# A two-layer hybrid decoder trunk: first stage in four blocks at once, pooling products later, transposes a tile behind, embedding weights loaded first

## The chip, the cores and the metric

The kernel runs on one core of a Trainium2 chip. The metric is device time in microseconds (us) from one launch. The engines are PE (TensorE, matmuls, with its weight loads PEld), DVE (VectorE), ACT (ScalarE), POOL (GpSimd) and SP (SyncE, which issues all DMAs). Each engine runs its own queue in order. Where an instruction waits for a semaphore, all that stands behind it in that queue waits too.

## The reference

All data are float32. The sequence has 1024 tokens of width 1024; there are two layers, one even and one odd.

```python
def reference(x, p, positions, norm_g, ple_w_gate, ple_w_proj, ...):
    h = x
    for i in range(DEPTH):                       # DEPTH = 2
        hn = rmsnorm(h, norm_g[i])
        m = even_layer(hn, ...) if i % 2 == 0 else odd_layer(hn, ...)
        h = h + m
        h = h + jax.nn.sigmoid(h @ ple_w_gate[i]) * (p[i] @ ple_w_proj[i])
    return h
```

The even layer multiplies the normalised input by one wide matrix, `ev_w_in`. The first 512 columns feed a pooling mixer: window means over 2, 4, 8 and 16 tokens minus the token, a small 64x64 product for each of four groups, a scale and a SiLU gate. The rest feeds six heads of differential attention: two softmaxes a head, subtracted with a factor lambda, with normalised and partly rotated queries and keys, an RMS norm and a gate. The odd layer has four heads of latent attention (low-rank queries and keys, `z = hn @ w_in` cut into 256 + 128 + 64 columns, normalised, multiplied up again) and four heads of a gated delta rule: a causal convolution, a triangular system of 64x64 per chunk (`solve(I + strict(kk * gamma * beta), [v*beta, k*beta*exp(gc)])`) and a recurrence over 16 chunks. After each layer comes a gated embedding, whose product `p[i] @ ple_w_proj[i]` is 1024x256 by 256x1024.

## The kernel before

The width or the tokens lie on 128 partitions, and an output tile is 128x512 (one bank of PSUM). Float32 products are made of three matmuls on a rounded high part and a low part of both operands: `mm3` (L141 to L144) issues high x high, high x low and low x high. `split` (L131 to L138) makes the parts: ACT casts the high part (L134, or L137 with a scale), DVE subtracts it (L135, or L138). `wload` (L151) loads 128x512 weight tiles through a pool of four raw buffers and splits them; the DMA is L158. `proj_T` and `proj_tok` run over the eight (or two) pieces of the contracted dimension with `mm3`, so that a 128x512 output costs 24 matmuls (6 for the embedding).

PSUM banks come from small pools by name: `acc` (2), `s` (2), `x` (2), `tr` (1) and `o` (1). A tile that asks for a bank waits until the reader of the bank's last content is done.

A scheduler sets the order in each engine's queue when the kernel is built: it follows the dependences and its own estimate of when each result is ready, and not the order of the program. Generators (`even_proj`, `even_attn`, `ple_proj` and others) issue a piece of work per step, and `step(...)` advances them in turn; this gives the scheduler the pieces to interleave.

The first stage (L354 to L376) multiplies the input by the first 512 columns of `ev_w_in`, transposed: four output blocks of 128 columns (`first`, `second`), for the first and the second half of the tokens. The first half takes each of eight pieces `k` as it arrives and does 12 matmuls with it. The second half does three blocks and then the fourth with `proj_T`, on a bank of pool `acc`. Column sums of squares (L333) give the norm of each token through `token_rstd` (L178, ones-vector matmuls L182) and `token_row` (L185, a matmul L190 and a copy L191 that spread it along a row). `pool_in` (L345) multiplies a block with that row (L347, L350) and makes the gate (tanh L351, product L352). `even_pool` (L417) makes the window sums on POOL (L421), copies on ACT (L430), corrects them on DVE (L431 to L433) and multiplies by the group matrices on PE (L437). The head projections `even_proj` (L442) follow: four steps of two token tiles, each with one bank of `acc` that ACT and DVE read (L459 to L463; L463 is the last reader).

`ple_proj` (L579) makes the embedding product: it splits the inputs `pT`, then for each of two column groups loads two weight tiles and makes 8 outputs, each copied (L127) and stored (L595). `latent` (L750) makes the latent columns of a token tile: three activations (L760 to L764), a Newton iteration, two scalings (L771), three transposes on PE (L774) and their splits. `block_solve` (L983) inverts 32x32 triangular blocks for all chunks with 62 DVE operations (L994, L996) and stores them as `xinv` (L997); `gdn_solve` (L1002) reads blocks of it back into `U` (L1010) and assembles each 64x64 and 128x128 solution with small matmuls and copies. `mla_prep` (L1127) loads latent queries and keys as `zq` (L1135, L1136) and transposes them on PE (L1144).

Of the kernel before, what the change touches and what calls it, by code (L numbers as in the profile page):

```python
# [10 lines left out]
F32 = mybir.dt.float32  # L11
# [45 lines left out]
def trunk_kernel(ctx, tc, a, out, layers=2):  # L57
# [120 lines left out]
    def token_rstd(sums):  # L178

        ps = bank("o")  # L180
        for c in range(4):
            pe.matmul(ps[:, c:c + 1], sums[:, c * P:(c + 1) * P], ones[:, 0:1], start=True, stop=True)  # L182
        return mean_rsqrt(ps[:, 0:4], 4, D, "tok")

    def token_row(dst, cols, dg):  # L185
# [3 lines left out]
        ps = bank("o")  # L189
# [132 lines left out]
    def load_x(h, k, sums):  # L322
        raw = slots[h][k]
        dma.dma_start(raw, a["xT"][k * P:(k + 1) * P, h * 512:(h + 1) * 512])
        hi, lo = xt(), xt()
        split(hi, lo, raw, ng[:, k:k + 1])
        hn[k][h] = (hi, lo)
# [7 lines left out]
    def finish_x(h, sums):  # L335
        set_rstd(0, h, token_rstd(sums))
        token_row(rrow[h], rstd[0][:, 4 * h:4 * h + 4], T("sq", 3))
# [17 lines left out]
    first, w_pool = [bank(n) for n in ("acc", "acc", "s", "s")], []  # L355
    for k in range(KC):
        load_x(0, k, sums[0])
        w_pool += wload(a["ev_w_in"], 0, 512, row=k, nk=1)
        for j in range(4):
            q = slice(j * P, j * P + P)  # L360
            mm3(first[j], w_pool[k][0][:, q], w_pool[k][1][:, q], *hn[k][0], k == 0, k == KC - 1)
    second = [bank(n) for n in ("x", "x", "tr")]
    dma.dma_start(cst[:, P:C_END], a["cst"][:, P:C_END])
    for k in range(KC):
        load_x(1, k, sums[1])
        for j in range(3):
            q = slice(j * P, j * P + P)
            mm3(second[j], w_pool[k][0][:, q], w_pool[k][1][:, q], *hn[k][1], k == 0, k == KC - 1)
        if k == 2:
            finish_x(0, sums[0])  # L370
        if k > 3:
            pool_in(first[k - 4], k - 4, 0)
# [964 lines left out]
```

## Time and profile before

| what | value |
|---|---|
| median of 3 runs | 1472.44 us (1470.59 to 1477.74) |
| profiled execution | 1472.82 us |
| its span | 1471.1 us |
| mean granted clock of PE | 0.993 |
| busy: PE, DVE, ACT, POOL | 1415.7, 977.9, 664.6, 195.9 us |
| matmuls | 7447 |

A row of a timeline has the start in us from the span's start, the busy time in us, the engine, the source line, the operation, output and inputs with their shape, and in brackets how long the engine had been idle before it and what released it. `SPq` is the issue of a DMA by SP. A row of stretches has for each engine the busy time, then the granted clock of PE as a share of full, the share of time the DMA engines were busy, and GB/s. A waits row has the total in us, how often, and the longest.

### The profile page before, as it was taken

The page shows a single profiled execution, that of the slowest core. Times are in us where ns is not written, and L with a number is a line of the kernel's source. Part 1 is how long each engine was busy: PE and PEld are TensorE (multiplying, and loading weights), DVE is VectorE, ACT ScalarE, POOL GpSimd, SP SyncE. Part 2 cuts the span into 40 slices and gives each one's busy share as a digit, 9 for nine tenths or more (in the row PEclk, how much of TensorE's full clock was granted, in tenths as well). Part 3 has the DMA queues.
Part 4 walks back from the last instruction along what each step waited for, and adds up shares of the span by engine and source line. Part 5 has one row for each costly group of instructions (what it writes and reads, how often), then busy time and mean ns, then how long its engine had stood idle before and what let it go on. Part 6 is the DMA issues. An engine that isn't in the chain of part 4 may idle for free. (4 is left out here: it accounts for less than half of the span.)

```text
span 1471.1 us, 22586 instructions
## 1 busy us (share of the span) xinstructions
PE 1415.7 (96%) x7447; PEld 1153.8 (78%) x7447; DVE 977.9 (66%) x2853; ACT 664.6 (45%) x1662; POOL 195.9 (13%) x341
## 2 busy tenths in 40 slices
PE   8999999999999999999999999999989999999998
PEld 6677888888887778887777878778768888887876
DVE  6756766666667785366676788997557887633342
ACT  6335555565656732343554543434334455722220
POOL 0321101111011000022015621210000000000021
PEclk9999999999999999999999999999999999999999
DMA  6223424232333563333424433343676634443332
GB/s 225 61 70 103 108 51 108 51 108 51 101 101 99 160 200 109 108 121 119 103 70 165 181 107 102 99 134 110 214 250 195 204 124 135 129 137 104 126 108 86
DMA packets 127605, 181.51 MB, mean 123 GB/s; under 512 B 28393, under 2 KB 55297, under 8 KB 127489
## 3 DMA queue, kind: packets, MB, share of 16 engines
q1 hardware_dynamic: 127488, 180.08, 39.7%
q8 instruction: 59, 0.97, 0.3%
q14 instruction: 58, 0.47, 0.1%
HBM read 108.20 MB, written 52.95 MB: 110 GB/s over the span
## 5 line engine op out<-in xcount | busy, mean ns | idle before, releaser
L143 PE MATMUL acc<-wl,x 128*128 128x512 f32 (+1 forms) x576 | 229.5, 399 | 3.2 <-DVE wl L135 3.2
L142 PE MATMUL acc<-wh,x 128*128 128x512 f32 (+1 forms) x576 | 231.0, 402 | 0.7 <-DVE g L463 0.6
L144 PE MATMUL acc<-wh,x 128*128 128x512 f32 (+1 forms) x576 | 228.0, 396 | 0.0
L142 PE MATMUL acc<-x,wh 128*128 128x512 f32 x504 | 202.9, 403 | 6.1 <-ACT wh L134 4.6
L144 PE MATMUL acc<-x,wl 128*128 128x512 f32 x504 | 200.2, 399 | 3.6 <-DVE wl L135 3.3
L143 PE MATMUL acc<-x,wh 128*128 128x512 f32 x504 | 199.8, 397 | 0.0
L135 DVE TENSOR_TENSOR wl<-raw,wh 128x512 fp32r<-128x512 f32 (+2 forms) x184 | 124.5, 698 | 31.8 <-ACT wh L134 30.2
L134 ACT CAST wh<-raw 128x512 fp32r<-128x512 f32 (+2 forms) x184 | 105.9, 600 | 69.4 <-PE acc L143 22.6
L143 PEld LDWEIGHTS acc<-wl,x 128*128 128x128 f32 x576 | 109.2, 190 | 26.9 <-DVE wl L135 4.2
L142 PEld LDWEIGHTS acc<-wh,x 128*128 128x128 f32 x576 | 109.2, 190 | 24.4 <-DVE g L463 1.4
L144 PEld LDWEIGHTS acc<-wh,x 128*128 128x128 f32 x576 | 109.0, 189 | 22.5
L142 PEld LDWEIGHTS acc<-x,wh 128*128 128x128 f32 x504 | 94.9, 188 | 29.5 <-ACT wh L134 6.1
L144 PEld LDWEIGHTS acc<-x,wl 128*128 128x128 f32 x504 | 94.8, 188 | 29.5 <-DVE wl L135 7.4
L261 ACT ACTIVATE p<-p,mx 128x128 f32<-128x128 f32 (+7 forms) x128 | 99.4, 777 | 33.7 <-DVE mx L257 23.2
L143 PEld LDWEIGHTS acc<-x,wh 128*128 128x128 f32 x504 | 95.1, 189 | 21.6 <-issue 0.2
L674 POOL TENSOR_TENSOR u<-hp,hp 128x512 f32<-128x512 f32 x32 | 43.2, 1350 | 473.4 <-DVE hp L135 190.8
L144 PE MATMUL acc<-hp,wl 128*128 128x512 f32 x256 | 101.6, 397 | 0.6 <-DVE wl L135 0.6
L143 PE MATMUL acc<-hp,wh 128*128 128x512 f32 x256 | 101.6, 397 | 0.0
L142 PE MATMUL acc<-hp,wh 128*128 128x512 f32 x256 | 101.5, 396 | 0.0
L257 DVE CUSTOM_DVE_ANT_0 p<-s,cst 128x512 f32<-128x512 f32 (+3 forms) x128 | 74.2, 586 | 26.8 <-PE s L532 15.6
L672 DVE SCALAR_TENSOR_TENSOR th<-th,ld 128x512 f32<-128x512 f32 x32 | 30.0, 937 | 75.7 <-ACT th L670 75.7
L459 ACT ACTIVATE z<-acc,rstd 128x256 f32<-128x256 f32 x48 | 22.8, 475 | 101.3 <-PE acc L144 99.1
(554 smaller groups left out, 2866.4 us busy)
## 6 DMA issues: line engine op xcount, KB each, us to landing
raw<-in_ev_w_in SPq DMA_DIRECT2D x56, 256.0 KB
Q<-sq SPq DMA_DIRECT2D x96, 128.0 KB
qkv<-zz SPq DMA_DIRECT2D x16, 640.0 KB
raw<-cat SPq DMA_DIRECT2D x32, 256.0 KB
raw<-in_ple_w_gate SPq DMA_DIRECT2D x32, 256.0 KB
ld<-ple SPq DMA_DIRECT2D x32, 256.0 KB
zq<-qkv SPq DMA_DIRECT2D x16, 512.0 KB
K<-sq SPq DMA_DIRECT2D x48, 128.0 KB
```

The costliest lines, as they stand in the source:

```text
L134: s.copy(hi, src)
L135: v.tensor_tensor(out=lo, in0=src, in1=hi.bitcast(F32), op=ALU.subtract)
L142: pe.matmul(ps, lh, rh, start=first, stop=False)
L143: pe.matmul(ps, lh, rl, start=False, stop=False)
L144: pe.matmul(ps, ll, rh, start=False, stop=last)
L257: v.tensor_tensor_reduce(out=pm[:, c * 512:c * 512 + n], in0=ps[:, 0:n], in1=mk, scale=-scale, scalar=prev, op0=ALU.add, op1=ALU.min, accu ...
L261: s.activation(pm[:, 0:w], pm[:, 0:w], AF.Exp, bias=prev, scale=-1.0, accum_out=sums)
L459: s.activation(z[:, t % 4, :], ps[:, 0:256], AF.Identity, scale=rstd[0][:, t:t + 1])
L672: v.scalar_tensor_tensor(out=th, in0=th, scalar=1.0, in1=r, op0=ALU.add, op1=ALU.mult)
L674: g.tensor_tensor(out=u, in0=hi.bitcast(F32), in1=lo.bitcast(F32), op=ALU.add)
```

## The change

The second half of the first stage computes its four blocks together, 12 matmuls per piece, on banks of `x` (2), `tr` and `o`. Column sums go to `acc` and `s` instead of `o`, and the squares are taken one piece later. The lambda factor is computed after the first step of the head projections, and `even_pool` becomes a generator whose matmuls come after four steps of them. `ple_proj` loads and splits all four weight tiles before its first output, and the last even head takes more of it in. In the odd layer the first column sum is taken one output later; `latent` transposes tile c − 1 after tile c; the latent weights are loaded ahead of the rotation of the rotary key, and `decay` (the delta rule's decay factors) comes after two token tiles of queries and keys. In `gdn_solve` seven copies and negations go from DVE to ACT.

```diff
-    second = [bank(n) for n in ("x", "x", "tr")]
+    pool_ps = [[bank(n) for n in tags] for tags in (("acc", "acc", "s", "s"), ("x", "x", "tr", "o"))]
+    for h in range(2):
+        for k in range(KC):
+            load_x(h, k)
+            if h == 0:
+                w_pool += wload(a["ev_w_in"], 0, 512, row=k, nk=1)
+            if k:
+                square_x(h, k - 1, sums[h])
+            for j in range(4):
+                q = slice(j * P, j * P + P)
+                mm3(pool_ps[h][j], w_pool[k][0][:, q], w_pool[k][1][:, q], *hn[k][h], k == 0, k == KC - 1)
+            if h == 1 and k == 2:
+                finish_x(0, sums[0])
+            if h == 1 and k > 3:
+                pool_in(pool_ps[0][k - 4], k - 4, 0)
...
     finish_x(1, sums[1])
-    second.append(bank("acc"))
-    proj_T(hn, w_pool, 3, 1, second[3])
     for j in range(4):
-        pool_in(second[j], j, 1)
+        pool_in(pool_ps[1][j], j, 1)
...
         v.scalar_tensor_tensor(out=x[:, 32:L], in0=s4[:, 32:L], scalar=cst[:, C_IW + b:C_IW + b + 1],
                                in1=x[:, 32:L], op0=ALU.mult, op1=ALU.subtract)
+        yield
         for h in range(2):
             pm = bank("s")
...
+        w = [wload(a["ple_w_proj"][layer], 512 * gq, 512, nk=2) for gq in range(2)]
         yield
         for gq in range(2):
-            w = wload(a["ple_w_proj"][layer], 512 * gq, 512, nk=2)
...
-    step(ahead)
-    even_pool(0)
-    step(ahead)
-    even_pool(1)
-    step(ahead, ahead)
+    pools_ = [even_pool(b) for b in range(2)]
+    step(pools_[0], ahead)
...
+    step(ahead, pools_[0], pools_[1], ahead, ahead, pools_[1])
...
-        step(at, at, ahead, late, done, at, at, ahead, at, at, ahead, at, ahead, at, at)
+        if hd < 5:
+            step(at, at, ahead, late, done, at, at, ahead, at, at, ahead, at, ahead, at, at)
+        else:
+            step(at, at, ahead, ahead, late, done, at, ahead, at, at, ahead, at, ahead, at, ahead, at, ahead, at, ahead)
...
-                if more and gq == 1:
-                    set_rstd(1, h, token_rstd(sums[h]))
+                    if more and gq == h == 1 and j == 1:
+                        set_rstd(1, 0, token_rstd(sums[0]))
+        if more:
+            set_rstd(1, 1, token_rstd(sums[1]))
...
+            zs.append(z)
+            if c:
+                transposes(c - 1)
+        transposes(3)
...
-        v.tensor_copy(W[32:64], ps[32:64, 0:P])
-        v.tensor_copy(W[96:128], ps[96:128, 0:P])
+        s.copy(W[32:64], ps[32:64, 0:P])
+        s.copy(W[96:128], ps[96:128, 0:P])
...
-        v.tensor_copy(W2[64:128], ps[64:128, 0:256])
+        s.copy(W2[64:128], ps[64:128, 0:256])
...
-        v.tensor_scalar(U3[0:64, :, 64:128], c3(px[0:64, 0:256]), -1.0, None, ALU.mult)
+        s.activation(U3[0:64, :, 64:128], c3(px[0:64, 0:256]), AF.Identity, scale=-1.0)
...
+    we = latent_weights()
     krt = T("gz", 2, pool=bp).rearrange("p (t o d) -> p t o d", o=1, d=64)
     rope(g, kr.unsqueeze(2), krt, cos1, sin1, 1, 32)
-    decay()
-    we = latent_weights()
...
-    for _ in range(NT):
+    for t in range(NT):
         step(qkvs, gp0, qkvs)
+        if t == 1:
+            decay()
```

What this does to the queues, at three places. Lines of the changed kernel differ by a few from those above.

On SP, around the second embedding product, before. `ple` are stored outputs (L595), `raw` the weight tiles; these are the third and fourth of them.

```order
L595 DMA ple_2_1_120<-ple_11559 128x512 [waits DMAHW4_49,Activation_49]
L595 DMA ple_3_0_121<-ple_11569 128x512 [waits DMAHW5_49,Activation_49]
L158 DMA raw_11588<-in_ple_w_proj 128x512 [waits DMAHW6_49,DMAHW2_49]
L595 DMA ple_3_1_122<-ple_11579 128x512 [waits DMAHW7_49,Activation_49]
L158 DMA raw_11594<-in_ple_w_proj 128x512 [waits DMAHW4_49,DMAHW0_49]
```

On SP, the same loads in the changed kernel, all four, behind the last input load (`in_pT`).

```order
L148 DMA raw_11205<-in_pT 128x512 [waits DMAHW0_49,Activation_49]
L158 DMA raw_11209<-in_ple_w_proj 128x512 [waits DMAHW1_49,DVE_49]
L158 DMA raw_11215<-in_ple_w_proj 128x512 [waits DMAHW2_49,DVE_49]
L1151 DMA zq_11301<-qkv_7626 128x4x256 [waits DMAHW3_49]
L158 DMA raw_11221<-in_ple_w_proj 128x512 [waits DMAHW7_49,DMAHW4_49,DVE_49]
L158 DMA raw_11227<-in_ple_w_proj 128x512 [waits DMAHW5_49,DMAHW0_49,DVE_49]
L1152 DMA zq_11300<-qkv_7626 128x4x256 [waits DMAHW6_49]
```

The loads moved ahead of all product stores, and two of them between the two `zq` loads of a head.

On DVE, at the end of the first stage, before. `g_628` and `pt_629` belong to the rotary tables, `p_847` holds window sums, `acc_786` is the first bank of the head projections.

```order
L352 SCALAR_TENSOR_TENSOR Q_182<-z_620,Q_182 128x512 [waits Activation_49]
L352 SCALAR_TENSOR_TENSOR Q_182<-z_624,Q_182 128x512 [waits Activation_49]
L206 TENSOR_SCALAR g_628<-g_628 128x64 [waits DVE_49]
L135 TENSOR_TENSOR wl_779<-raw_777,wh_778 128x512 [waits DMAHW0_49]
L207 TENSOR_TENSOR g_628<-g_628 128x64 [waits DVE_49]
L212 TENSOR_SCALAR g_628<-g_628 128x64
L431 TENSOR_TENSOR p_847<-p_847,cst 128x16 [waits Pool_49]
L433 SCALAR_TENSOR_TENSOR p_180<-p_847,cst,p_180 128x1008
L213 SCALAR_TENSOR_TENSOR pt_629<-g_628 128x64 [waits DVE_49]
L432 TENSOR_TENSOR p_180<-p_847,p_180 128x16 [waits DVE_49]
```

On DVE, the same place in the changed kernel (L426 to L428 were L431 to L433, L354 was L352, L459 was L463).

```order
L426 TENSOR_TENSOR p_729<-p_729,cst 128x16 [waits Activation_49,Pool_49]
L428 SCALAR_TENSOR_TENSOR p_180<-p_729,cst,p_180 128x1008 [waits DVE_49]
L354 SCALAR_TENSOR_TENSOR Q_182<-z_622,Q_182 128x512 [waits Activation_49]
L354 SCALAR_TENSOR_TENSOR Q_182<-z_626,Q_182 128x512 [waits Activation_49]
L206 TENSOR_SCALAR g_630<-g_630 128x64 [waits DVE_49]
L427 TENSOR_TENSOR p_180<-p_729,p_180 128x16 [waits DVE_49]
L207 TENSOR_TENSOR g_630<-g_630 128x64 [waits DVE_49]
L212 TENSOR_SCALAR g_630<-g_630 128x64
L459 SCALAR_TENSOR_TENSOR g_789<-th_816,acc_790 128x128 [waits PE_49,Activation_49]
```

The weight splits (L135) are gone from here, since they stand earlier; the window products moved ahead of the gate products, and the reader of the bank stands right behind both.

On PE, in the latent stage, before: the transposes of the fifth tile's `gz` stand inside the matmuls of the sixth (`acc_8067`).

```order
L144 MATMUL acc_8067<-wh_7739,x_7505 128x456
L774 MATMUL tr_8057<-cst,gz_8032 128x128 [waits DVE_49,Activation_49]
L774 MATMUL tr_8057<-cst,gz_8032 128x128
L142 MATMUL acc_8067<-wh_7745,x_7545 128x456
L774 MATMUL tr_8057<-cst,gz_8032 128x128 [waits DVE_49]
```

On PE, the same tile's transposes in the changed kernel, with the end of the sixth tile's matmuls ahead of them.

```order
L142 MATMUL acc_8059<-wh_7753,x_7588 128x456
L143 MATMUL acc_8059<-wl_7754,x_7588 128x456
L144 MATMUL acc_8059<-wh_7753,x_7589 128x456
L769 MATMUL tr_8109<-cst,gz_8034 128x128 [waits DVE_49,Activation_49]
L769 MATMUL tr_8109<-cst,gz_8034 128x128
L769 MATMUL tr_8109<-cst,gz_8034 128x128 [waits DVE_49]
L142 MATMUL acc_8119<-wh_7711,x_7070 128x456
```

The group moved six matmuls later, behind the sixth tile.

More of the change, by code (lines that the diff above doesn't have):

```diff
@@ L176, in proj_T, with token_rstd @@
             mm3(ps, w[k][0][:, sl], w[k][1][:, sl], xh, xl, i == 0, i == len(ks) - 1)
-    def token_rstd(sums):
-        ps = bank("o")
+    def token_rstd(sums, tag="o"):
+        ps = bank(tag)
         for c in range(4):
@@ L320, in trunk_kernel, with load_x, square_x @@
              [T("v", 4) for _ in range(4)] + [t[:, 512 * i:512 * i + 512] for t in [T("p0", 2, (PW[0],)) for _ in range(2)] for i in range(2)]]
-    def load_x(h, k, sums):
+    def load_x(h, k):
+        dma.dma_start(slots[h][k], a["xT"][k * P:(k + 1) * P, h * 512:(h + 1) * 512])
+        hi, lo = xt(), xt()
+        split(hi, lo, slots[h][k], ng[:, k:k + 1])
+        hn[k][h] = (hi, lo)
+    def square_x(h, k, sums):
         raw = slots[h][k]
[L324 to L327, printed above, removed]
         if k == 0:
@@ L335, in finish_x @@
     def finish_x(h, sums):
-        set_rstd(0, h, token_rstd(sums))
-        token_row(rrow[h], rstd[0][:, 4 * h:4 * h + 4], T("sq", 3))
+        set_rstd(0, h, token_rstd(sums, ("acc", "s")[h]))
+        token_row(rrow[h], rstd[0][:, 4 * h:4 * h + 4], T("sq", 3), ("acc", "s")[h])
     L = T_ + 16
@@ L354, in trunk_kernel @@
     sums = [T("o", 2) for _ in range(2)]
[L355 to L361, printed above, removed]
-    second = [bank(n) for n in ("x", "x", "tr")]
[L363 to L372, printed above, removed]
+    w_pool = []
+    pool_ps = [[bank(n) for n in tags] for tags in (("acc", "acc", "s", "s"), ("x", "x", "tr", "o"))]
[13 more added lines that the diff above has]
+                pool_in(pool_ps[0][k - 4], k - 4, 0)
+        square_x(h, KC - 1, sums[h])
+        if h == 0:
+            for j in range(2):
+                raw = px[j][:, 16:528]
+                s.copy(raw, pool_ps[0][j])
+                pool_ps[0][j] = raw
+            dma.dma_start(cst[:, P:C_END], a["cst"][:, P:C_END])
     finish_x(1, sums[1])
-    second.append(bank("acc"))
-    proj_T(hn, w_pool, 3, 1, second[3])
     for j in range(4):
-        pool_in(second[j], j, 1)
+        pool_in(pool_ps[1][j], j, 1)
     rtmp = T("g", 3, (3, 64))
@@ L592, in ple_proj @@
                     ps, t = bank("acc"), outs()
[L593 removed]
+                    proj_T(pT, w[gq], j, h, ps)
                     copy(h * (1 - layer), t, ps)
@@ L606, in trunk_kernel @@
     ahead = even_proj(0, st)
-    step(ahead)
-    even_pool(0)
-    step(ahead)
-    even_pool(1)
-    step(ahead, ahead)
+    pools_ = [even_pool(b) for b in range(2)]
+    step(pools_[0], ahead)
+    lvt = T("o", 2)[:, 0:256]
+    dma.dma_start(lvt, a["ev_lambda"].rearrange("o a b -> (o a b)").partition_broadcast(P))
+    neglam = yp.tile([P, 1], F32, name="neglam")
+    ld, le = S("ld", 2), S("le", 2)
+    for i in range(2):
+        v.tensor_tensor_reduce(out=lvt[:, 128 * i:128 * i + 64], in0=lvt[:, 128 * i:128 * i + 64],
+                               in1=lvt[:, 128 * i + 64:128 * i + 128], scale=1.0, scalar=0.0,
+                               op0=ALU.mult, op1=ALU.add, accum_out=ld[:, i:i + 1])
+    s.activation(le, ld, AF.Exp)
+    v.scalar_tensor_tensor(out=neglam, in0=le[:, 1:2], scalar=-LAM_INIT, in1=le[:, 0:1], op0=ALU.add, op1=ALU.subtract)
+    step(ahead, pools_[0], pools_[1], ahead, ahead, pools_[1])
     done = iter(())
@@ L753, in latent, with transposes @@
             la[k][h] = (lat[k][:, 0:512], lat[k][:, 512:1024])
+        zs = []
+        def transposes(c):
+            cc = slice(c * P, c * P + P)
+            tr = bank("tr")
+            for k in range(3):
+                pe.transpose(tr[:, k * P:(k + 1) * P], zs[c][:, k * P:(k + 1) * P], ident)
+            for k in range(3):
+                hi, lo = la[k][h]
+                split(hi[:, cc], lo[:, cc], tr[:, k * P:(k + 1) * P])
         for c in range(4):
             t = 4 * h + c
-            cc = slice(c * P, c * P + P)
             ps = bank("acc")
```

26 lines of the change are left out of this document (4 added, 22 removed).

## The prediction

> **What bounds the kernel now.** I read the busy table first, then busy time by stretch, then the waits of PE, then the engines around each wait in order of time.
>
> ```profile
> span 1471.1 us, 22586 instructions
> PE 1415.7 (96%) x7447; PEld 1153.8 (78%) x7447; DVE 977.9 (66%) x2853; ACT 664.6 (45%) x1662; POOL 195.9 (13%) x341
> 50.00:75.00 25.00, 21.83 (x85) 16.22 (x84) 22.60 (x47) 10.75 (x20) 13.18 (x10) 0.93 0.29 85
> 475.00:500.00 25.00, 22.49 (x128) 17.81 (x127) 20.89 (x84) 17.33 (x50) 0.00 (x0) 1.00 0.45 127
> 500.00:525.00 25.00, 22.58 (x123) 17.67 (x123) 18.53 (x47) 18.00 (x37) 0.00 (x0) 1.00 0.73 233
> 1050.00:1075.00 25.00, 21.93 (x106) 18.20 (x105) 22.06 (x51) 11.52 (x20) 1.03 (x3) 0.93 0.81 263
> 1075.00:1100.00 25.00, 20.31 (x129) 15.49 (x127) 10.80 (x50) 8.03 (x17) 0.00 (x0) 0.86 0.68 233
> 1100.00:1270.00 170.00, 166.03 (x1474) 144.35 (x1472) 136.07 (x558) 87.64 (x194) 5.04 (x12) 1.00 0.51 155
> ```
> PE is busy 1415.7 of 1471.1 us: TensorE bounds the kernel nearly throughout, and a change that leaves its matmuls alone can only win back its 55 us of idle time and the time at a lowered clock. In the stretch rows stand the length, busy time by engine (PE first) and then the granted clock: of 25 us PE is idle 3.2, 2.5, 2.4, 3.1 and 4.7 in five stretches that the change rewrites, and the clock is 0.93 and 0.86 of full in three of them. A clock of 0.93 over 25 us is 1.7 us lost, if PE is busy. From 1100 to 1270 PE is idle only 4.0 of 170 us.
>
> No matmul of any size is added or removed, so I price the change by stalls: which wait goes, and what is late next. The sum stands against the profiled execution, 1472.82 us; the median of the three runs, 1472.44, is 0.4 below it.
>
> **E. The second embedding projection: four weight tiles loaded first.**
>
> ```profile
> 1035.66 0.63 SPq L1136 DMA_DIRECT2D zq<-qkv  x1
> 1051.13 0.60 PE L1144 MATMUL s<-cst,zq 128*128 128x128 f32 x4
> 1055.24 1.09 PE L1144 MATMUL s<-cst,zq 128*128 128x128 f32 x4 [3.07 <-DMA zq<-qkv]
> 1075.72 0.33 SPq L158 DMA_DIRECT2D raw<-in_ple_w_proj  x1
> 1078.95 0.33 SPq L158 DMA_DIRECT2D raw<-in_ple_w_proj  x1
> 1080.10 0.62 ACT L134 CAST wh<-raw 128x512 fp32r<-128x512 f32 x1 [3.77 <-DMA raw<-in_ple_w_proj]
> 1080.77 0.80 PE L142 MATMUL acc<-pT,wh 128*128 128x512 f32 x1 [4.19 <-ACT wh L134]
> 1086.34 0.50 PE L142 MATMUL acc<-pT,wh 128*128 128x512 f32 x1 [0.49 <-ACT ple L127]
> 1079.39 0.37 SPq L997 DMA_DIRECT2D xinv<-nx  x1
> 1083.43 0.32 SPq L1010 DMA_DIRECT2D U<-xinv  x1
> 1089.02 0.43 SPq L1010 DMA_DIRECT2D U<-xinv  x1
> ```
> The third and fourth tiles are issued on SP only at 1075.72 and 1078.95, behind stores of finished products, which wait for ACT's copies. ACT converts at 1080.10, PE stands 4.19 us, then 0.49, and the clock of the stretch is 0.86: 3.5 us of 25, of which some 1.2 lay inside the idle time, so 2.3 on PE. Together 7.0 us. The new order issues all four loads right behind the input loads. What they pass on SP: two of them now stand ahead of the second `zq` load of a head (L1136), which was issued at 1035.66 for transposes at 1051.13. Those 15 us cover two loads of 256 KB and the release of a buffer: no cost. The `zq` load that PE waits 3.07 us for at 1055.24 waits for a buffer that PE's own transposes free; that stall stays.
>
> What is late next is the triangular inverse: its store is issued at 1079.39, the first of its blocks is read back at 1083.43, and the fourth is issued at 1089.02, behind product stores that themselves wait for the stalled matmuls. In the new order five operations of the inverse's chain on DVE stand ahead of the K and Q splits instead of between them, and the product stores between the read-backs wait for matmuls that no longer stall. I put the store 1.5 us sooner and the fourth read-back about 4 us behind the first, so some 5.5 us earlier than now, while PE comes 7.0 earlier. PE had no wait there, so 0 to 1.5 us come back. **E saves 6.5 us**; 7.0 at the upper end; at the lower end the read-back is as late as now and returns 4.5, which leaves 2.5.
>
> **A. The first stage: second half in four blocks, 12 matmuls a step.**
>
> ```profile
> 30.76 0.40 PE L142 MATMUL x<-x,wh 128*128 128x512 f32 x1
> 45.46 0.69 DVE L352 SCALAR_TENSOR_TENSOR Q<-z,Q 128x512 f32<-128x512 f32 x1 [0.16 <-ACT z L351]
> 49.68 0.95 PE L182 MATMUL o<-cst,o 128*128 128x1 f32 x8
> 55.65 1.10 PE L190 MATMUL o<-sq,cst 128*128 128x512 f32 x2
> 57.60 0.69 DVE L347 TENSOR_TENSOR p<-x,g 128x512 f32<-128x512 f32 x1
> 60.62 2.41 POOL L421 TENSOR_TENSOR p<-p 64x1038 f32<-64x1038 f32 x1
> 63.10 2.25 POOL L421 TENSOR_TENSOR p<-Q 128x1039 f32<-128x1039 f32 x1
> 62.01 3.89 DVE L352 SCALAR_TENSOR_TENSOR Q<-z,Q 128x512 f32<-128x512 f32 x2 [0.76 <-ACT z L351]
> 66.66 0.50 PE L143 MATMUL acc<-wl,x 128*128 128x512 f32 x1 [3.15 <-DVE wl L135]
> 68.85 1.98 DVE L215 COPY pt<-pt 128x64 f32<-128x64 f32 x1
> 70.81 0.27 DVE L463 SCALAR_TENSOR_TENSOR g<-th,acc 128x128 f32<-128x128 f32 x1
> 73.44 1.88 PE L437 MATMUL s<-p,pw 128*128 128x512 f32 x4
> ```
> Now the fourth block comes behind the other three (the column sums L182 at 49.68 stand ahead of it) and holds the weight buffers to 57. DVE, stuck 3.89 us in two L352 that take 0.69 each elsewhere, splits the last weight late: PE stands 3.15 us at 66.66, then loses the 1.7 of the clock. In the new order the buffers come free as the second half goes, and all eight weight splits stand ahead of the row products on DVE. That stall goes.
>
> What is late next: from 30.76 to 49.68 there are 72 matmuls and two small steps (0.95 and 1.10 us, like the rows of L182 and L190): 0.234 us each. The new second half has 96 and ends at 55.3; with one more L182 the projection starts at 56.1 and, with L190 inside its first block, wants its third accumulator at 68.4. L190 comes 15 matmuls into it, at 59.6 instead of 55.65. So the row products L347, and POOL's window sums behind them, come 3.95 us later: POOL's second sum ends at 67.0, its third at 69.3. On DVE the window products (L431 to L433) now stand ahead of the two L352, and all of these ahead of L463, which frees the accumulator. L431 needs POOL's second sum, 67.0. But the L352 at 62.01 was held until the third sum ended (65.35), though POOL had a gap of 0.07 us between the two; so I take 69.3. Then L431 to L433 (1.4), two L352 (1.3) and three small ones (0.4) give L463 at 72.4, and PE resumes at 72.7. In the old order the same progress stands at 73.45: the third accumulator follows the L437 of 73.44, four records in 1.88 us, of which 1.3 are PE's time and come later in the new order, so 74.75 − 1.3. The stage is 0.75 ahead there, but PE has stood 4.3 us, and I charge one slow stretch for it, 1.7. **A costs 1.0 us.** If DVE is let in at 67.0, PE resumes at 70.4: a gain of 3.0. If L212 ahead of L463 is held too, as L215 was for 1.98 us at 68.85, PE resumes at 74.8 with two slow stretches in part: a loss of 3.5.
>
> The row of L352 meets a rule of the Trainium skill, page "SBUF — State Buffer", section "Who interferes with whom": a DVE instruction with two SBUF inputs and a GpSimd instruction that reads SBUF shut each other out, and the later one blocks fully. The trace agrees, with 3.89 us for two L352. By the same section an instruction with one SBUF input is free outside the 2-port modes; L212 would then not be held and A stays at 1.0, while the row of L215, with one input, shows a hold and would give 3.5.
>
> **C. Latent stage: transposes a tile behind, rope and decay later.**
>
> ```profile
> PE o L182 <- DVE sums L687: 1.6, 2, 1.0
> PE tr L774 <- DVE gz L771: 1.6, 5, 0.5
> 722.84 0.21 ACT L870 ACTIVATE ea<-alog 128x4 f32<-128x4 f32 x1 [2.60 <-DMA alog<-in_od_a_log]
> 725.57 0.55 PE L774 MATMUL tr<-cst,gz 128*128 128x128 f32 x3 [1.89 <-DVE z L135]
> 759.60 1.31 POOL L242 TENSOR_TENSOR kr<-kr,gz 128x512 f32<-128x512 f32 x1
> 759.70 1.76 DVE L135 TENSOR_TENSOR nx<-raw,cv 128x512 fp32r<-128x512 f32 x1
> 761.52 0.50 PE L143 MATMUL x<-nx,z 128*128 128x512 f32 x1 [1.58 <-DVE nx L135]
> ```
> The first two rows give all waits of a kind: us in total, times, the longest. The order on PE moves little: each of the eight groups of transposes stays within six matmuls of its place. The 1.89 at 725.57 hangs on ACT, where L870 waits for a small load until 722.84 with the splits of the transposes behind it; L870 keeps its place, so this stays, with its slow stretch. The 1.58 at 761.52 is DVE's split held beside POOL's rope (1.76 us); both keep their places too. What goes: the smaller of the two waits for column sums, 0.6, since that sum moves behind ten more matmuls; and of the five waits of L774 for L771, 1.6 in all, the two where a group moves six matmuls (1.2 us) later, 0.9. **C saves 1.5 us**; 0 if the waits only move; 3.5 if decay's departure from DVE frees the 1.58 as well.
>
> **B. Last head of the even layer.** 64 matmuls of the first embedding projection move from behind the last head into it. PE is idle 4.9 us from 475 to 525 (the two rows above); these matmuls' weights are loaded at the same place on SP as now. They close a gap only where one stands just ahead of it: between 0 and 4. **B saves 2.0 us**, the middle.
>
> **D. Solver copies from DVE to ACT.**
>
> ```profile
> L1045 DVE COPY wk<-acc 64x256 f32<-64x256 f32 x8 | 3.4, 428 | 2.5 <-PE acc L1044 2.2
> L277 ACT COPY pt<-tr 128x256 f32<-128x256 f32 x3 | 1.1, 373 | 2.7 <-PE tr L275 2.7
> ```
> Seven copies in each of eight solves leave DVE. ACT takes 0.37 us for 128x256 where DVE takes 0.43 for 64x256, so a copy costs about the same. DVE is busy 80% of 1100 to 1270, ACT 52%, but PE waits 4.0 us there in all. On ACT the copies queue behind softmax pieces. At best a third of the 4.0 goes, 1.5; at worst half as much is added, 2.0. **D: 0**, the middle.
>
> Sum: −6.5 + 1.0 − 1.5 − 2.0 + 0 = −9.0. 1472.8 − 9.0 is 1463.8; for a median 0.4 below, 1463.4.
>
> **Rivals.**
> *First stage gains.* DVE is let in when POOL's second sum ends: A is −3.0, the time 1459.4. For it: L463 did get in at 70.81, right behind the held L215. Against it: the held L352.
> *Gain given back.* PE waits for the inverse's read-back: E is −2.5, the time 1467.4. For it: a chain on DVE and two trips through memory, not the weights, set 1089.02. Against it: the stores ahead of it go sooner with PE.
> *Only E counts.* B and C keep their waits in other places: 1466.9. For it: the transposes hardly move.
> *Slower: the solver's handoffs.* A solve has three steps of PE, copy, PE in series, and on ACT each copy may stand behind a softmax piece. There are 24 such handoffs; if PE has nothing to run meanwhile, 0.38 us each eats the 9.0, and from 0.7 each the kernel is slower by over 0.5%: 24 times 0.7 is 16.8, which gives 1480.2. Against it: attention work stands between the steps, and PE was idle only 2.4% there.
>
> **Chances and range.** Forecast 0.43, first stage gains 0.20, gain given back 0.17, only E 0.11, slower 0.09. A measurement here tells about 0.5% (7.4 us) from no change, so faster means under 1465.1. The forecast's own spread puts it there 8 times in 10 and the first rival always; of the next two one in eight does; the last is slower 7 times in 9. Faster 0.58, same 0.35, slower 0.07. All good ends together give 1453, all bad ones 1476, and neither is likely; 1456 to 1471 holds the first four cases with their bounds.
>
> **What would show it.** E: the two waits for weight casts gone, a clock near 1.00 from 1070 to 1090, and under 1.5 us of waiting at the first solve. A: a wait of some 4 us for L463's analog near 68 to 73. C: the 1.89 and 1.58 still there. D: PE idle near 4 us from 1100 to 1270. The prediction is wrong if the third accumulator comes free by 69, if the fourth read-back is issued near 1089, or if 1100 to 1270 has over 4 us more of idle time.

## The result and the profile after

The changed kernel took 1461.57 us (median of 7 runs, 1460.56 to 1464.81), the kernel before 1471.37 us (median of 7, 1469.85 to 1477.74): a ratio of 0.9926, 95% interval 0.9913 to 0.9939. The forecast was 1463.4 us. The profiled execution after took 1462.1 us with a span of 1460.4 us and a mean granted clock of 0.996.

The head of its page:

```profile
span 1460.4 us, 22616 instructions
PE 1407.7 (96%) x7447; PEld 1150.0 (79%) x7447; DVE 956.6 (66%) x2797; ACT 680.7 (47%) x1720; POOL 192.9 (13%) x341
```

The same stretches as before, with 1025 to 1050 added (length; busy time of PE, PEld, DVE, ACT, POOL; granted clock; DMA share; GB/s):

```profile
50.00:75.00 25.00, 21.98 (x92) 17.09 (x91) 18.01 (x45) 8.24 (x17) 8.66 (x9) 0.95 0.16 43
475.00:500.00 25.00, 22.73 (x130) 18.15 (x129) 19.95 (x78) 16.62 (x48) 0.00 (x0) 1.00 0.47 137
500.00:525.00 25.00, 24.68 (x137) 20.00 (x136) 18.15 (x50) 16.28 (x37) 0.00 (x0) 1.00 0.66 215
1025.00:1050.00 25.00, 21.54 (x101) 17.36 (x99) 13.18 (x34) 7.16 (x13) 0.53 (x1) 0.98 0.68 213
1050.00:1075.00 25.00, 23.71 (x100) 19.32 (x101) 20.38 (x50) 9.97 (x17) 1.03 (x3) 0.89 0.82 258
1075.00:1100.00 25.00, 23.30 (x214) 18.61 (x213) 7.61 (x48) 13.28 (x35) 1.14 (x3) 1.00 0.67 224
1100.00:1270.00 170.00, 166.06 (x1443) 145.07 (x1442) 122.59 (x508) 104.08 (x244) 3.87 (x9) 1.00 0.50 157
```

The stretch 1075 to 1100 is repaired (23.30 busy at full clock for 20.31 at 0.86), and so is 500 to 525 (24.68 for 22.58). What is left idle in the first are two waits of 0.85 us for ACT's copies of products (L127), at 1079.08 and 1081.60. In its place the slow stretch ahead of it has grown: 0.89 from 1050 to 1075, where it was 0.93, and 1025 to 1050 shows 3.5 us idle. Three waits of PE are new or have moved. First, the first stage, in order of time:

```profile
65.73 1.91 POOL L416 TENSOR_TENSOR p<-p 64x1038 f32<-64x1038 f32 x1
67.68 0.17 DVE L426 TENSOR_TENSOR p<-p,cst 128x16 f32<-128x16 f32 x1 [1.91 <-POOL p L416]
67.72 1.92 POOL L416 TENSOR_TENSOR p<-Q 128x1039 f32<-128x1039 f32 x1
67.77 2.94 DVE L428 SCALAR_TENSOR_TENSOR p<-p,cst,p 128x1008 f32<-128x1008 f32 x1
72.42 0.29 DVE L459 SCALAR_TENSOR_TENSOR g<-th,acc 128x128 f32<-128x128 f32 x1
72.77 0.79 PE L142 MATMUL acc<-wh,x 128*128 128x512 f32 x1 [3.02 <-DVE g L459]
```

PE resumes at 72.77; the forecast was 72.7. It has waited 3.02 us, where the forecast had 4.3. DVE did get in when POOL's second sum ended (L426 at 67.68), but the next one, L428, was then held beside the third sum for 2.94 us, so the bank's reader L459 came no sooner. Second, the start of the even output stage, in the kernel before (one row) and in the changed one:

```profile
533.89 0.69 DVE L654 TENSOR_TENSOR t<-acc,ld 128x512 f32<-128x512 f32 x1 [0.58 <-DMA ld<-in_xT]
```

```profile
534.33 0.69 DVE L661 TENSOR_TENSOR t<-acc,ld 128x512 f32<-128x512 f32 x1 [1.05 <-DMA ld<-in_xT]
535.08 0.50 PE L142 MATMUL acc<-x,wh 128*128 128x512 f32 x1 [3.33 <-DVE t L661]
```

L661 (L654 before) adds the residual, whose load lands at about 534, as late as before; PE now comes to that point sooner and waits 3.33 us. Third, ahead of the embedding product:

```profile
1045.39 0.59 ACT L1161 CAST K<-s 128x512 fp32r<-128x512 f32 x1 [9.54 <-PE s L1160]
1047.31 1.30 ACT L926 ACTIVATE gz<-acc,hrstd 128x512 f32<-128x512 f32 x2
1046.01 0.69 DVE L1162 TENSOR_TENSOR K<-s,K 128x512 fp32r<-128x512 f32 x1 [3.79 <-ACT K L1161]
1050.43 0.69 DVE L927 SCALAR_TENSOR_TENSOR gz<-gz,acc 128x512 f32<-128x512 f32 x1
1051.18 0.80 PE L142 MATMUL acc<-wh,x 128*128 128x512 f32 x1 [4.64 <-DVE gz L927]
```

ACT stands idle 9.54 us in front of the casts of K (L1161), which wait for PE's transposes; behind them in its queue stands the reader of a gate product (L926, twice). DVE's part L927 follows behind four splits and pieces of the inverse. Only then is the bank free for which PE has waited 4.64 us. Before, the first transposes of the second half of the tokens stood ahead of that gate product on PE, and the wait at this place was 3.07 us.

Last, the waits of PE in the latent stage (us in all, how often, the longest), before (four kinds, beyond those shown ahead) and after:

```profile
PE acc L144 <- DVE wl L135: 1.1, 1, 1.1
PE s L142 <- DVE zz L816: 1.0, 1, 1.0
PE tr L142 <- DVE zz L816: 0.5, 1, 0.5
PE o L875 <- DVE gd L872: 0.3, 1, 0.3
```

```profile
PE x L143 <- DVE nx L135: 1.7, 1, 1.7
PE o L892 <- ACT zz L837: 1.4, 1, 1.4
PE acc L144 <- DVE wl L135: 0.9, 1, 0.9
PE tr L769 <- DVE z L135: 0.8, 1, 0.8
PE o L182 <- DVE sums L694: 0.7, 1, 0.7
PE tr L769 <- DVE gz L790: 0.6, 1, 0.6
```

### The profile page after: what moved, and what is told of

It is laid out like the page before. It is cut to its first block, busy times and chain, and to the rows that moved or that the text cites. A ratio compares the mean times of both kernels' runs of the same rounds, so it can differ in the third digit from the quotient of the medians.

```text
span 1460.4 us, 22616 instructions
## 1 busy us (share of the span) xinstructions
PE 1407.7 (96%) x7447; PEld 1150.0 (79%) x7447; DVE 956.6 (66%) x2797; ACT 680.7 (47%) x1720; POOL 192.9 (13%) x341
## 5 line engine op out<-in xcount | busy, mean ns | idle before, releaser
L142 PE MATMUL acc<-x,wh 128*128 128x512 f32 x496 | 199.2, 402 | 8.6 <-ACT wh L134 4.9
L144 PE MATMUL acc<-x,wl 128*128 128x512 f32 x496 | 197.0, 399 | 3.1 <-DVE wl L135 2.9
L143 PE MATMUL acc<-x,wh 128*128 128x512 f32 x496 | 196.6, 397 | 0.0
L135 DVE TENSOR_TENSOR wl<-raw,wh 128x512 fp32r<-128x512 f32 (+2 forms) x184 | 123.1, 691 | 29.2 <-ACT wh L134 26.4
L142 PEld LDWEIGHTS acc<-x,wh 128*128 128x128 f32 x496 | 93.4, 189 | 31.5 <-ACT wh L134 6.3
L143 PEld LDWEIGHTS acc<-x,wh 128*128 128x128 f32 x496 | 93.6, 189 | 20.8
```

The source lines that it names most:

```text
L135: v.tensor_tensor(out=lo, in0=src, in1=hi.bitcast(F32), op=ALU.subtract)
L142: pe.matmul(ps, lh, rh, start=first, stop=False)
L143: pe.matmul(ps, lh, rl, start=False, stop=False)
L144: pe.matmul(ps, ll, rh, start=False, stop=last)
```

## Where the time went, stage by stage

PE issues the same 7447 matmuls in every kernel. The table gives the time from PE's n-th matmul to its m-th in the profiled execution of each of the fourteen kernels, worked out from the traces: 100 to 500 is the first stage (part A of the prediction), 2310 to 2600 the last even head (B), 3200 to 4000 the latent stage (C), 4860 to 5100 the second embedding product (E), 5100 to 6640 the solver and the scan, where D lies. In 1600 to 2310 no kernel differs. The ratio is that to the kernel before, timed beside it (half-widths of the 95% intervals 0.0009 to 0.0015).

| kernel | parts | 100–500 | 1600–2310 | 2310–2600 | 3200–4000 | 4860–5100 | 5100–6640 | 6640–7446 | ratio |
|---|---|---|---|---|---|---|---|---|---|
| before | none | 97.1 | 138.3 | 60.3 | 184.9 | 53.0 | 180.8 | 185.9 | 1 |
| changed | ABCDE | 98.5 | 136.5 | 60.3 | 178.8 | 50.1 | 178.8 | 185.8 | 0.9926 |
| A undone | BCDE | 97.1 | 136.7 | 58.8 | 178.5 | 48.3 | 178.6 | 185.6 | 0.9933 |
| C undone | ABDE | 98.3 | 137.9 | 59.1 | 182.1 | 49.1 | 178.6 | 186.1 | 0.9965 |
| D undone | ABCE | 98.3 | 137.9 | 58.4 | 179.6 | 49.1 | 183.1 | 185.4 | 0.9964 |
| E undone | ABCD | 98.3 | 136.5 | 60.8 | 178.2 | 53.1 | 182.1 | 189.4 | 0.9989 |
| E alone | E | 97.0 | 136.5 | 60.0 | 181.1 | 48.6 | 182.1 | 186.3 | 0.9965 |
| D alone | D | 97.0 | 136.5 | 61.4 | 184.0 | 54.9 | 180.5 | 186.1 | 1.0002 |
| C alone | C | 97.3 | 136.1 | 59.9 | 180.6 | 52.9 | 181.1 | 185.9 | 0.9965 |
| E and C | CE | 97.1 | 136.4 | 59.1 | 180.8 | 48.8 | 183.2 | 185.2 | 0.9954 |
| E, C and D | CDE | 97.4 | 136.4 | 58.9 | 180.3 | 48.8 | 178.6 | 186.5 | 0.9931 |
| no residual | ABCDE | 98.4 | 136.4 | 56.5 | 178.0 | 49.1 | 178.8 | 187.2 | 0.9928 |
| gate on bank o | ABCDE | 98.3 | 138.1 | 58.5 | 178.2 | 51.5 | 181.8 | 186.7 | 0.9990 |
| gates first | ABCDE | 98.1 | 136.4 | 59.7 | 178.3 | 44.4 | 179.5 | 186.4 | 0.9920 |

The unchanged column shows how far one trace can be trusted: ten kernels take 136.1 to 136.7 us, four take 137.9 to 138.3. The difference is one slow stretch of the clock, which comes or stays away. So each part is read from the means of the kernels that have it against those that have not (the three kernels with edits of their own left out where their edit lies).

The columns 4860–5100 and 5100–6640 do not hold the same matmuls in every kernel, since scores move from one to the other. Counted by the columns of their outputs, at 0.234 us for 512, the first of the two has about 0.6 us more work in the kernel before than in the changed one, 1.1 more in "gates first" and 2.7 more in "gate on bank o" (estimates). The two added up can be compared safely: 233.8 us before, 228.9 in the changed kernel, 224.0 and 233.3 in those two.

## The experiments

**A undone.** The first stage, the pooling and the lambda factor as before.

```diff
-    pool_ps = [[bank(n) for n in tags] for tags in (("acc", "acc", "s", "s"), ("x", "x", "tr", "o"))]
+    second = [bank(n) for n in ("x", "x", "tr")]
...
+    second.append(bank("acc"))
+    proj_T(hn, w_pool, 3, 1, second[3])
```

> The changed kernel (1461.6 us) with the first stage, the pooling and the lambda factor as before. Theory 1, from the two traces: the new first stage costs 1.9 us by the 500th matmul; without it the time is 1459.7. Theory 2, the prediction's term: it costs 1.0; 1460.6. Rival: the part gains (its long stall goes and the clock stays up), 1464.5 or more. In the trace the wait of 3.02 us at 72.77 for L459 should be gone and the one of 3.15 for the last weight split be back.

Measured: 1459.33 us beside 1470.14 for the kernel before, 0.9933 (0.9919 to 0.9947), not to be told from the changed kernel's 0.9926. Its stage takes 97.1 us. Over all kernels it is 98.31 us with A (seven, 98.1 to 98.5) and 97.15 without (seven, 97.0 to 97.4). The time from the 500th to the 1600th matmul, not in the table, is longer with A as well, 208.7 us for 208.2 (208.6 to 208.8 and 208.2 to 208.3). So by the traces the part costs 1.6 us, 1.2 of them in its stage; the rival that it gains falls. The whole time is too coarse to show it.

**E undone.** Two weight tiles per column group again.

```diff
-        w = [wload(a["ple_w_proj"][layer], 512 * gq, 512, nk=2) for gq in range(2)]
         yield
         for gq in range(2):
+            w = wload(a["ple_w_proj"][layer], 512 * gq, 512, nk=2)
```

> The changed kernel with two weight tiles of the embedding product loaded per column group, as before (both layers). Theory 1, from the traces: this part is worth 2.9 us, since a new wait of 4.64 us at 1051 for the gate reader L927 takes part of it; 1464.5. Theory 2, the prediction's term: 6.5 us; 1468.1. Rival: the new wait at 1051 hangs on this part, and goes with it; then the two are even, about 1462.

Measured: 1467.85 us, 0.9989 (0.998 to 0.9998): 0.0063 above the changed kernel, 9.3 us of 1470. That is more than either theory said. Its own stage is 3.0 us longer than the changed kernel's, which fits the first theory; but the solver and scan are longer too (182.1 for 178.8), and so is the end (189.4 for 185.8). The end is not the part's: the profiled execution is the slowest of the twelve (1471.82 us), with a wait of 1.77 us for a weight cast and a slow stretch at 1329.

**C undone.** Column sum, transposes, latent weights and decay as before.

```diff
-            zs.append(z)
-            if c:
-                transposes(c - 1)
-        transposes(3)
+            tr = bank("tr")
+            for k in range(3):
+                pe.transpose(tr[:, k * P:(k + 1) * P], z[:, k * P:(k + 1) * P], ident)
```

> The changed kernel with the column sum, the latent transposes, the latent weights and decay as before. Theory 1, from the traces: this part is worth 6.1 us; 1467.7, with the wait of 1.89 us before the transposes near 725, a slow stretch behind it, and the four small waits for gz back. Theory 2, the prediction's term: 1.5 us; 1463.1. Rival: most of the 6.1 is the slow stretch, which comes or not by chance of its phase; then 1464 to 1465.

Measured: 1465.17 us, 0.9965 (0.9953 to 0.9977), 5.7 us above the changed kernel. In its trace the wait before the transposes is 1.18 us and no slow stretch follows; the stage is still 3.3 us longer. So more than the 1.5 of the prediction is the part's own.

**D undone.** The solver's copies on DVE again.

```diff
-        s.copy(W2[64:128], ps[64:128, 0:256])
+        v.tensor_copy(W2[64:128], ps[64:128, 0:256])
```

> The changed kernel with the solver's copies and negations on DVE again. Theory 1, from the traces: the part is worth 2.0 us between 1140 and 1200; 1463.6. Theory 2, the prediction's term: nothing; 1461.6 within 0.5. Rival: copies on ACT cost time that another part hides; 1460 or less.

Measured: 1464.51 us, 0.9964 (0.9952 to 0.9976), 5.6 us above the changed kernel; the solver and scan take 183.1 us for 178.8. From 1095 to 1200 PE's longest wait in this kernel, and in the changed one:

```profile
PE acc L1161 <- DVE K L1163: 1.7, 1, 1.7
```

```profile
PE x L1138 <- DVE od L1137: 0.9, 2, 0.8
```

With the copies on DVE, the split of K for the next head (L1163) comes late; with them on ACT that wait does not show. Both theories are too low. The four parts undone one by one sum to 9.3 + 5.7 + 5.6 + 1.0 = 21.6 us, twice what the change brings, so they are not independent. The next three make one part at a time on the kernel before.

**E alone.**

```diff
+        w = [wload(a["ple_w_proj"][layer], 512 * gq, 512, nk=2) for gq in range(2)]
         yield
         for gq in range(2):
-            w = wload(a["ple_w_proj"][layer], 512 * gq, 512, nk=2)
```

> The kernel before (1470.1 us beside it) with only the embedding weights loaded first. Theory 1, from the parts undone one by one: the part wins 3 to 4.7 us up to the solver and the solver and scan, which then keep their copies on DVE, lose 2; 1467 to 1469. Theory 2, the prediction's term: 6.5 us; 1463.6. Rival, from the kernel with this part undone: it is worth 9 by itself; 1461.

Measured: 1465.92 us beside 1470.54, 0.9965 (0.9952 to 0.9978), 5.1 us less. The stage gives 4.4 and the solver and scan take 1.3 back in the trace. The same wait as in the changed kernel stands at 1051.68: 4.64 us for the gate reader. So that wait belongs to E.

**D alone.**

```diff
-        v.tensor_copy(W[32:64], ps[32:64, 0:P])
+        s.copy(W[32:64], ps[32:64, 0:P])
```

> The kernel before with only the solver's copies and negations on ACT. Theory 1: the parts need each other; alone this one wins nothing, since the solver and scan with these copies on ACT but the old weight order took 1 us longer than before; 1470 to 1472. Theory 2, the prediction's term: nothing; 1470.1 within 0.5. Rival, from the kernel with this part undone: 5.6 us by itself; 1464.5.

Measured: 1470.71 us, 1.0002 (0.9989 to 1.0015). Alone it brings nothing, as the first theory and the prediction's own term said.

**C alone.**

```diff
+            zs.append(z)
+            if c:
+                transposes(c - 1)
+        transposes(3)
...
+    we = latent_weights()
     krt = T("gz", 2, pool=bp).rearrange("p (t o d) -> p t o d", o=1, d=64)
```

> The kernel before with only the later column sum, latent transposes, latent weights and decay moved. Theory 1: 3.3 us from the waits for gz, the column sums and the smaller one near 724, and up to 3 more where a slow stretch no longer follows that wait; 1464 to 1467. Theory 2, the prediction's term: 1.5; 1468.6.

Measured: 1466.23 us, 0.9965 (0.9953 to 0.9977), 5.1 us less, in the range of the first theory.

**E and C.** The two diffs above together.

```diff
+        w = [wload(a["ple_w_proj"][layer], 512 * gq, 512, nk=2) for gq in range(2)]
...
+            if c:
+                transposes(c - 1)
```

> The kernel before (about 1470.3 us) with the embedding weights first and the latent stage changed, and nothing else. Theory 1: these two are the whole change, and their savings add (5.1 and 5.1 when made alone); 1460.2, as fast as the changed kernel. Theory 2: without the solver's copies on ACT the weights' part gives some back in the solver, as in the kernel with that part undone; 1463 to 1465, with 71.5 to 72.5 us from record 5100 to 5800 of PE where the changed kernel takes 69.5.

Measured: 1463.03 us beside 1469.45, 0.9954 (0.9941 to 0.9967): the second theory. PE's records 5100 to 5800 take 71.85 us; the changed kernel takes 69.46. From 5100 to 6640 the kernels with E and without D take 182.8 us (three), with D and without E 181.3 (two), with neither 180.9 (two), and with both 178.7 (five, within 0.2). D is worth 4.1 us where E is there and nothing where it is not. PE's idle time that DVE ended goes the same way: 3.3 to 5.1 us with E and without D, 1.9 to 2.1 with both, 2.5 and 2.7 with neither. The order on PE shows what E does to the solver: in the kernel before, two groups of attention scores stand inside the embedding product, ahead of the first solve; with the weights early, one score matmul stands there, the rest of its group just ahead of the first solve, and the next groups between the solver's steps.

**E, C and D.** The changed kernel with the first stage and the last head as before.

```diff
-        if hd < 5:
-            step(at, at, ahead, late, done, at, at, ahead, at, at, ahead, at, ahead, at, at)
-        else:
-            step(at, at, ahead, ahead, late, done, at, ahead, at, at, ahead, at, ahead, at, ahead, at, ahead, at, ahead)
+        step(at, at, ahead, late, done, at, at, ahead, at, at, ahead, at, ahead, at, at)
```

> The changed kernel (about 1459.4 us here) with the first stage and the last even head as before. Theory 1: the first stage costs 1.2 us and the last head saves 0.8, so 1459.0: the same within what can be measured. Rival: the first stage is worth nothing and the head 2.0, as predicted; 1461.4.

Measured: 1459.28 us, 0.9931 (0.992 to 0.9943), the same as the changed kernel: within the 1.8 us that the interval leaves on either side, these three parts are the change.

**No residual.** The first two output blocks of the even layer leave the residual out.

```diff
-                    t, r = T("t", 2), T("ld", 2)
-                    dma.dma_start(r, res[jj][h])
-                    v.tensor_tensor(out=t, in0=ps, in1=r, op=ALU.add)
+                    t = T("t", 2)
+                    if layer == 0 and gq == h == 0 and j < 2:
+                        v.tensor_copy(t, ps)
```

> The changed kernel with the residual left out of the first two output blocks of the even layer (and their two loads). Theory 1: the wait of 3.33 us at 535 is a wait for that load alone and gives back what the last head had gained; without it 2 to 2.8 us less, about 1457. Rival: another operand is as late there (the weights or the splits), and the wait only changes its name; 1459.4.

Measured: 1458.22 us, 0.9928 (0.9914 to 0.9943). The stretch with the wait, in the changed kernel and then here:

```profile
525.00:550.00 25.00, 21.67 (x93) 17.15 (x93) 21.07 (x52) 8.16 (x14) 1.36 (x1) 1.00 0.57 181
```

```profile
525.00:550.00 25.00, 25.00 (x109) 20.13 (x108) 22.70 (x60) 6.64 (x11) 2.58 (x1) 1.00 0.47 154
```

PE is never idle there now, and the stage takes 56.5 us; the kernels with B take 59.36 (seven, 58.4 to 60.8), those without 59.94 (six, 58.9 to 61.4). So the wait is for the residual load alone, as the first theory said, and hides 2.9 us. The whole time does not show it: that ratio's interval spans 4 us, and the end of this trace is 1.5 us longer.

**Gate on bank o.** The last tile of the second gate product asks for another bank.

```diff
-            ps = bank("acc")
+            ps = bank("o" if i == 1 and t == 7 else "acc")
             proj_tok(hn1, w, t, 512, ps)
```

> The changed kernel with the last tile of the second gate product on the bank of pool o instead of acc, so that it need not wait for the gate reader L927. Theory 1: the wait of 4.64 us at 1051 is a wait for that bank alone; it goes, and the clock stays up in the embedding product: 4 to 5 us less than the changed kernel, about 1455. Rival: the embedding's first block asks for the same bank a few us later, or the transposes wait for their zq load instead: 1 us less at most, about 1458.5.

Measured: 1468.8 us beside 1470.54, 0.999 (0.9977 to 1.0004): 9 us slower than the changed kernel, far from both. The wait only moved (first fence), and there is a new slow stretch (second):

```profile
1056.35 0.50 PE L142 MATMUL acc<-pT,wh 128*128 128x512 f32 x1 [3.92 <-DVE gz L927]
```

```profile
1165.00:1180.00 15.00, 14.51 (x128) 11.44 (x126) 9.16 (x46) 8.32 (x23) 0.00 (x0) 0.89 0.47 144
```

It is not the bank but the late reader, as the rival said. And in the new order four groups of scores stand ahead of the solver's first steps; the solver and scan take 181.8 us for 178.8, with a slow stretch at 1165 to 1180. That is more than it looks, since some 2.7 us of its work have moved into the stage ahead; the two together take 233.3 us for 228.9. The trace accounts for 5.6 of the 9 us; most other runs of this kernel were longer than the profiled one.

**Gates first.** Two tiles of the gate product are stepped ahead of the loads of `zq`.

```diff
-    step(ahead, gp1, gp1, ahead, gp1, ahead, gp1, ahead, gp1)
+    step(gp1, gp1, ahead, gp1, ahead, gp1, ahead, gp1, ahead)
```

> The changed kernel with two tiles of the second gate product stepped ahead of the latent queries' and keys' loads, so that the gate readers stand ahead of the casts of K and Q on ACT and DVE. Theory 1: the wait of 4.64 us at 1051 is made by that queue order; it goes, with one slow stretch: 48 to 46 us or less from record 4860 to 5100 (now 50.1), and the solver keeps its time; 1454 to 1456. Rival: the scores move ahead of the first solver steps with it, as with the other bank, and the solver and scan give 3 us or more back; 1458 to 1462.

Measured: 1457.52 us beside 1469.45, 0.992 (0.9907 to 0.9933), the lowest ratio of all. The gate readers on ACT, and the stretches:

```profile
1038.88 0.69 ACT L926 ACTIVATE gz<-acc,hrstd 128x512 f32<-128x512 f32 x1 [3.37 <-PE acc L144]
1044.48 0.69 ACT L926 ACTIVATE gz<-acc,hrstd 128x512 f32<-128x512 f32 x1 [4.91 <-PE acc L144]
1046.61 0.59 ACT L1161 CAST K<-s 128x512 fp32r<-128x512 f32 x1 [0.81 <-PE s L1160]
```

```profile
1025.00:1050.00 25.00, 24.64 (x114) 19.61 (x113) 14.57 (x37) 9.20 (x16) 1.36 (x4) 1.00 0.71 210
1050.00:1075.00 25.00, 23.87 (x112) 19.30 (x111) 18.48 (x47) 10.37 (x18) 0.19 (x1) 1.00 0.95 303
1075.00:1100.00 25.00, 25.00 (x277) 20.54 (x275) 10.91 (x65) 15.49 (x44) 1.67 (x4) 1.00 0.72 218
```

Each reader now follows its own product at once (1038.88, 1044.48; the pair stood at 1047.31), ahead of the casts. The 4.64 us are gone and the clock is at 1.00 throughout: the stage takes 44.4 us for 50.1. So the wait was made by the order of ACT's and DVE's queues. Of the 5.7 us the solver and scan return 0.8, which leaves 4.9, and the end 0.6. By the ratios this kernel is ahead of the changed one by 0.0006, less than their intervals; that it is faster is shown for the stage, not for the whole.

## Why the prediction came out

The total was right: 9.0 us forecast, 9.8 measured by the medians. The parts were not, and that their errors cancel is luck: E, B and A together fell 4.0 us short of the forecast, C and D went 4.5 beyond it. Each as forecast, and as the means of the kernels with and without it give:

| part | forecast | measured |
|---|---|---|
| E, weights first | −6.5 | −4.5 (48.98 with, eight; 53.47 without, four) |
| A, first stage | +1.0 | +1.6 (+1.2 in its stage, the rest up to the 1600th matmul) |
| C, latent stage | −1.5 | −3.9 (179.11 with, ten; 183.03 without, four) |
| B, last head | −2.0 | −0.6 (less than the spread between kernels, 2.4) |
| D, solver's copies | 0 | −2.1 in the solver and scan (178.7 with D and E; 180.9 with neither) |
| sum | −9.0 | −9.5 |

- **A** was right in its place (72.77 for 72.7) and in what holds PE there, and near in its size. The wait is shorter than the 4.3 us forecast: the column sums (L182) that end the half stand at 56.55 and not at 55.3, so PE comes to the bank at 69.75 and not at 68.4. One step was right for a wrong reason: I took 69.3 for DVE's start because L352 had been held at 62.01 until the third sum ended. That row is two instructions. By itself, the first came through when the second sum ended (60.62 and 2.41 us, so 63.03), and only the second was held to the end of the third:

```profile
62.01 1.57 DVE L352 SCALAR_TENSOR_TENSOR Q<-z,Q 128x512 f32<-128x512 f32 x1 [0.76 <-ACT z L351]
63.50 2.40 DVE L352 SCALAR_TENSOR_TENSOR Q<-z,Q 128x512 f32<-128x512 f32 x1
```

  In the changed kernel it is the same: DVE started at 67.68 and was held one instruction later, at the same cost. So the argument that the prediction held against its rival "first stage gains" was a misreading, and that the place came out is luck: DVE came in early and lost it again.
- **E**: the mechanism was right. The two waits for weight casts are gone, 1075 to 1100 is at full clock, and PE does not wait at the first solve. The term was mis-sized because I wrote "that stall stays" of the 3.07 us at 1055.24. I looked at the `zq` load, and not at the order on PE, where the gate product came ahead of the transposes; the stall became 4.64 us with a slow stretch of 6.8 us. "Gates first" shows its price, 5.7 us of the stage. The rival that the inverse's read-back gives the gain back did not come: the fourth read-back is issued at 1083.38, where the prediction had about 1083.5.
- **C**: I counted waits of two kinds and got 1.5. The column sums gave 0.9 of waits and the transposes' waits for gz 1.0 of 1.6. That "this stays" of the 1.89 us at 725.57 was the failed step: the wait is 1.89, 1.64, 1.18, 0.87, 0.77 and less in kernels whose order there is the same or nearly so, since it hangs on the landing of a small load. The kernel before, in its profiled execution, had the longest, and the slow stretch behind it. In all, PE is idle 5.8 us of the stage with the part and 8.5 without (means of the same kernels): 2.7 of the 3.9. The rest is no idle time in the records. PE waits 7 or 8 times in the stage with the part, 13 or 14 times without; a row of a matmul lasts 0.40 us and the next starts 0.23 after it (1039.96 and 1040.19 in the changed kernel), so a wait costs up to 0.17 us more than its listed time: an estimate of 1.0 us for six.
- **B**: the waits inside the head went as forecast (500 to 525: 24.68 busy for 22.58), but I named nothing that is late next. It is the residual load, and it returns most of it; whether anything is left is not shown, as the kernels' spread is larger.
- **D**: nothing alone, as forecast. I did not ask what D is worth beside E. E moves scores into the solver, PE then waits more for DVE there (3.3 to 5.1 us for 2.5 and 2.7), and D takes copies off DVE (1.9 to 2.1).

Of the rivals, "first stage gains" and "gain given back" by the inverse are refuted, "only E counts" too (E alone gives half), and the solver's handoffs on ACT cost nothing. What the forecast said would be seen: the two cast waits gone, yes; a wait of some 4 us at L459 near 68 to 73, yes (3.02); the 1.58 still there, yes (1.7); the 1.89 still there, no (0.8); 4 us idle from 1100 to 1270, yes (3.9), although that row could not show the solver's gain, since it does not hold the same matmuls (1474 before, 1443 after). None of the three signs of being wrong came.

Of the difference of the two traces, 10.7 us of their spans, 1.7 us are luck: the trace before has a slow stretch at 471 to 474.5 which ten of the fourteen kernels lack in the same code.

## What to carry to other kernels

Where parts share a queue, take each out of the changed kernel and also put each alone on the old one: here the four taken out summed to twice the whole. When a stall goes, look up the next load or reader that PE will meet and when it is ready, for an unchanged arrival (the residual at 534) takes the gain. Have the reader of an accumulator stand in its engine's queue right behind the matmuls that fill it, ahead of anything that waits for later matmuls: that was worth 5.7 us of a stage, 4.9 with the one behind it, and cost one line.

## What the runs showed of the hardware

**The length of a wait alone does not decide whether a slow stretch follows.** The same wait of 1.71 us and then the stretch behind it, before (two fences) and in the changed kernel (two more):

```profile
470.81 0.47 PE L491 MATMUL x<-cst,z 128*128 128x128 f32 x1 [1.71 <-POOL z L242]
```

```profile
471.00:474.50 3.50, 3.50 (x19) 3.50 (x19) 0.92 (x3) 0.18 (x2) 0.00 (x0) 0.53 0.01 2
```

```profile
472.88 0.33 PE L487 MATMUL x<-cst,z 128*128 128x128 f32 x1 [1.71 <-POOL z L242]
```

```profile
473.00:476.50 3.50, 3.50 (x29) 3.31 (x30) 1.45 (x7) 1.72 (x8) 0.00 (x0) 1.00 0.00 0
```

After the one the clock is 0.53 for 3.5 us, after the other 1.00; a slow stretch costs 1.7 us. The Trainium skill, page "TensorE: Matmul & The Clock Gate", section "HAM oscillation — how this bites in real kernels", gives as the rule that no idle gap should be longer than about 3.4 us. Here a gap of half that was followed by the lower clock and an equal one was not, so for gaps of this size the rule does not tell.

The clock records of the fourteen traces show more. In each trace the changes of the clock lie on a grid of 3.41 us, and a slow stretch lasts one or two of its steps. Of the 47 slow stretches between 30 and 1450 us, 39 follow a step in which PE was idle for 1.77 us or more in all; of the other 5714 steps at full clock one was idle that long (idle time as the records give it). In the kernel before, the 1.71 us lie in one step, which ends at 470.85 and has 1.84 us of idle time; in the changed kernel a step ends at 472.03, in the middle of the wait. So was the wait of 3.33 us at 535 divided, into 1.7 and 1.6, and no slow stretch followed it, while in "gates first" a step with 2.44 us of idle time at the same place, ending at 533.83, was followed by one. Eight slow stretches came after less idle time (0.5 to 1.6 us), and why is open. The grid lies differently from trace to trace, so for a wait of about 1.7 to 3.5 us (twice 1.77, an estimate) it hangs on the place of the grid whether a slow stretch follows.

**DVE beside POOL.** In the changed kernel L428 took 2.94 us while POOL's sum ran (rows above) and 1.26 at another place, with POOL idle:

```profile
81.33 1.26 DVE L428 SCALAR_TENSOR_TENSOR Q<-p,cst,Q 128x1008 f32<-128x1008 f32 x1
74.38 1.91 DVE L212 TENSOR_SCALAR g<-g 128x64 int32<-128x64 f32 x1
72.19 0.19 DVE L212 TENSOR_SCALAR g<-g 128x64 int32<-128x64 f32 x1
```

L212, with one input, took 0.19 us at 72.19 and 1.91 at 74.38, with POOL busy, so an instruction with one input is held here too, against the reading in the prediction that L212 would not be. In these two cases the price was about the time that POOL's instruction had left (L428 began at 67.77 and took 1.68 us longer, and POOL's sum ran from 67.72 for 1.92 us; at 74.28 another one had just begun), and not a share of DVE's own.
